# GpSimd makes the lower part of eleven expert weights, and three float32 units become split ones

## The chip, the core and the metric

The kernel runs on one core of a Trainium2 chip. The metric is the time of one execution on the device, in microseconds (us). TensorE multiplies matrices, VectorE and ScalarE do elementwise work, GpSimd is a fourth compute engine, and SyncE issues the transfers. Each engine works through its own instructions in a fixed order and waits at semaphores for the others.

## The reference, cut to what matters

Two transformer blocks over 256 tokens of width 1024, in float32. The change lies in the feed-forward part of the first block, a product-key mixture of 16384 experts:

```python
def chunk(xc):                       # 128 tokens
    q = (xc @ w_query).reshape(128, 8, 2, 128)
    s1 = einsum('thd,hnd->thn', q[:, :, 0], sub_keys_1)
    s2 = einsum('thd,hnd->thn', q[:, :, 1], sub_keys_2)
    v1, i1 = top_k(s1, 16); v2, i2 = top_k(s2, 16)
    cand = v1[..., :, None] + v2[..., None, :]        # 16 x 16 per head
    best, pos = top_k(cand, 16)
    idx = take_along_axis(i1 * 128 + i2, pos)         # experts chosen
    g = softmax(best)
    act = gelu(einsum('td,thkd->thk', xc, expert_u[idx]))
    return einsum('thk,thkd->td', g * act, expert_v[idx])
```

## The kernel before, in words

The kernel gathers nothing. It computes x @ u for all 16384 experts, in 64 units of 256 experts (`unit_u`, line 544 on: the u units), builds the gate values as a dense matrix out of one-hot products, and multiplies the gated activations with all of expert_v.

A matmul in full float32 precision is had in two ways. `wstat` (line 230 on) takes weights that are split into an upper part, which is the weight rounded to float32r, and a lower part, which is the rest, also as float32r. It does three matmuls for each of 16 blocks: upper by upper activations, upper by lower activations, lower by upper activations (lines 240 to 242), 48 in all. `wstat_f32` (line 245 on) uses the unsplit weight in 32 float32 matmuls (line 252) on the float32 activations `xf`, and no other engine works for it.

The split is `load_split` (line 68): a 1 MB transfer on SyncE's queue into one of three buffers `w` (line 71), a copy on ScalarE that makes the upper part (line 77), and a subtraction on VectorE that makes the lower part (line 78). Upper and lower parts have two buffers each, shared by query weights and u units in turn, so the split of a weight waits until the weight two before it has been used up. `load_ahead` does the split earlier than its use, `fetch` takes what lies ready.

The selection stage follows the first block's attention. For each of eight heads `query(h)` does: a 1 MB query weight q by `wstat`, ScalarE copies the result (qT), one u unit, the scores against the keys (sc, line 607), a copy of them to SBUF (scs, lines 613 to 615). `select(h - 1, ...)` then finds the previous head's top 16 on VectorE by max, find and replace steps (lines 583 to 587), adds up the candidates (cand, line 624) and takes the top 16 again. Head 1 has a float32 unit (u0); heads 2 to 7 have split ones (u1 to u6).

The tail of the stage, behind the loop: unit u7 (float32), u8 (split), the last `select`, index arithmetic on VectorE and ScalarE (pi, pf, ij: lines 650 to 658), u9 (split), and for each half of the tokens a lookup by comparison (lines 666 to 671: ScalarE broadcasts `eq`, VectorE compares, multiplies and adds up in a tree), each followed by a float32 unit (u10, u11). A softmax lies between. Then the indices are transposed (tsel, line 684), and 16 steps follow that each take one split u unit (u12 on) and build one-hot tiles on VectorE (oh, lines 706 to 709) for the one-hot matmuls (gp, line 714).

What sets the order: the text of the kernel gives each instruction a priority, earlier text first; a planner runs through them ahead of time with costs of its own, gives each engine the first instruction in priority that is ready then, and so fixes the order on each engine. An instruction that is late in the text can therefore stand early on an engine, where the planner saw a gap. GpSimd has no instruction in this stage.

Of the kernel before, what the change touches and what calls it, by code (L numbers as in the profile page):

```python
# [10 lines left out]
F32 = mybir.dt.float32  # L11
# [37 lines left out]
def kernel(ctx: ExitStack, tc: tile.TileContext, A: dict, out: bass.AP):  # L49
    nc = tc.nc  # L50
    V, S, PE, GP = nc.vector, nc.scalar, nc.tensor, nc.gpsimd
# [10 lines left out]
    def mm_tile(name):  # L62
        return mmp.tile([P, 512], F32, tag="mm", name=name)
# [1 line left out]

    last_split = []

    def load_split(src, n, name, after=(), dst=None):

        w = strm.tile([P, 2048], F32, tag="w", name=name, bufs=3)  # L70
        nc.sync.dma_start(w[:, :n], src)
        hi, lo = dst or [strm.tile([P, 2048], F32R, tag="w" + z, name=f"{name}{z[0]}") for z in ("hi", "lo")]
        with ExitStack() as queued:
            for i in after:
                queued.enter_context(tc.issue_after(i.ins))
            last_split[:] = [
                S.activation(hi[:, :n], w[:, :n], AF.Copy),  # L77
                V.tensor_sub(lo[:, :n], w[:, :n], hi[:, :n].bitcast(F32)),  # L78
            ]
        return hi, lo  # L80

# [89 lines left out]

    ahead = {}

    def load_ahead(src, n, name, after=(), dst=None):
        if name not in ahead:
            ahead[name] = load_split(src, n, name, after, dst)

    def queued(after, f, *a, **kw):

# [5 lines left out]
    def fetch(src, n, name):  # L185
        return ahead.pop(name) if name in ahead else load_split(src, n, name)
# [43 lines left out]
    def wstat(xh, xl, src, name, pool=mm_tile, at=None):  # L230

        hi, lo = fetch(src, 2048, name)
        ps = pool(name + "p")
        for j in range(2):
            for k in range(8):
                if at is not None and j == 0 and k == 4:
                    at()
                c = slice(k * 256 + j * P, k * 256 + j * P + P)
                o = ps[:, j * T : j * T + T]
                PE.matmul(o, hi[:, c], xh[:, k], start=k == 0, stop=False)  # L240
                PE.matmul(o, hi[:, c], xl[:, k], start=False, stop=False)
                PE.matmul(o, lo[:, c], xh[:, k], start=False, stop=k == 7)
        return ps

    def wstat_f32(xf, src, name):

        w = strm.tile([P, 2048], F32, tag="w", name=name, bufs=3)
        nc.sync.dma_start(w, src)
        ps = mm_tile(name + "p")
        for j in range(2):  # L250
            for k in range(8):
                PE.matmul(ps[:, j * T : j * T + T], w[:, k * 256 + j * P : k * 256 + j * P + P], xf[:, k], start=k == 0,
                          stop=k == 7)
        return ps
# [278 lines left out]
    with tc.tile_pool(name="p2", bufs=1) as p2, tc.tile_pool(name="gdram", bufs=1, space=bass.MemoryType.DRAM) as gdp:  # L533
# [7 lines left out]
        gact = {}  # L541
        nu = [0]

        def unit_u(n=1, xf=None):
            for _ in range(n):
                j = nu[0]
                if j == 64:
                    return
                nu[0] += 1
                ps = wstat(xh, xl, A["eu"][j], f"u{j}") if xf is None else wstat_f32(xf, A["eu"][j], f"u{j}")  # L550
                g = p2.tile([P, 512], F32, tag="ga", name=f"ga{j}", bufs=NG)
                S.activation(g, ps, AF.Gelu)
                gact[j] = g

        p2x = tc.tile_pool(name="p2x", bufs=1)
        xf = p2x.__enter__().tile([P, 8, T], F32, name="xf")
        with tc.tile_pool(name="p2a", bufs=1) as p2a:
            rs_f, pr = [], []

            def normed_x():  # L560

                rs_f.append(n_f.end())
                dg = p2a.tile([P, 2, P], F32, name="dgf")
                for t in range(2):
                    V.tensor_scalar(dg[:, t], ident, rs_f[0][:, t : t + 1], None, OP.mult)
                for k in range(8):
                    pt = mm_tile(f"ptn{k}")
                    for t in range(2):
                        PE.matmul(pt[:, t * P : t * P + P], x[t][:, k * P : k * P + P], dg[:, t], start=True, stop=True)
                    S.activation(xf[:, k], pt[:, :T], AF.Copy, scale=gcols[:, G_FFN + k : G_FFN + k + 1])  # L570

            def split_x():
                for k in range(0, 8, 2):
                    S.activation(xh[:, k : k + 2], xf[:, k : k + 2], AF.Copy)
                    V.tensor_sub(xl[:, k : k + 2], xf[:, k : k + 2], xh[:, k : k + 2].bitcast(F32))
# [13 lines left out]
            def query(h):  # L589
                ps = wstat(xh, xl, A["w_query"][h], f"q{h}", at=(lambda: pr.extend(n_f.half(1))) if h == 0 else None)  # L590
                if h == 0:
                    load_ahead(A["w_query"][1], 2048, "q1", pr)
                keys = p2a.tile([P, 2, P], F32, tag="keys", name=f"keys{h}", bufs=2)
                nc.sync.dma_start(keys, A["keys"][h])
                qT = p2a.tile([P, 512], F32, tag="qT", name=f"qT{h}", bufs=2)
                S.activation(qT, ps, AF.Copy)
                if h == 0:
                    normed_x()
                elif h == 1:
                    unit_u(1, xf)  # L600
                    split_x()
                else:
                    unit_u()
                s = mm_tile(f"sc{h}")
                for t in range(2):
                    for f in range(2):
                        PE.matmul(s[:, (2 * t + f) * P : (2 * t + f + 1) * P],
                                  qT[:, f * T + t * P : f * T + t * P + P], keys[:, f], start=True, stop=True)
                sc = p2a.tile([P, 4, P], F32, tag="sc", name=f"scs{h}", bufs=2)
                s = s.rearrange("p (a b) -> p a b", a=4)  # L610
                if h < 2:
                    for t in range(2):
                        S.activation(sc[:, 2 * t : 2 * t + 2], s[:, 2 * t : 2 * t + 2], AF.Copy, scale=rs_f[0][:, t : t + 1])
                else:
                    S.activation(sc, s, AF.Copy)
                return sc

            def select(h, sc):
                for t in range(2):
                    for f in range(2):  # L620
                        top16(sc[:, 2 * t + f], vals[:, t, f, h], idxu[:, t, f, h])
                cand = p2a.tile([P, 2, 112], F32, tag="cand", name=f"cand{h}", bufs=2)
                for o, i0, ni, nj in ((0, 0, 4, 16), (64, 4, 12, 4)):
                    V.tensor_tensor(
                        cand[:, :, o : o + ni * nj].rearrange("p t (i j) -> p t i j", i=ni),
                        vals[:, :, 0, h, i0 : i0 + ni].unsqueeze(3).to_broadcast((P, 2, ni, nj)),
                        vals[:, :, 1, h, 0:nj].unsqueeze(2).to_broadcast((P, 2, ni, nj)), OP.add)
                for t in range(2):
                    top16(cand[:, t], best[:, t, h], posu[:, t, h])

            prev = None
            for h in range(8):
                sc = query(h)
                if prev is not None:
                    select(h - 1, prev)
                prev = sc
            unit_u(1, xf)
            unit_u(1)
            select(7, prev)


# [14 lines left out]
            for a in range(2):  # L656
                V.tensor_mul(pf[2 + a], pf[2 + a], pf[4])
                V.tensor_add(ij[a].rearrange("p t h k -> p (t h k)"), pf[a], pf[2 + a])
            unit_u(1)
            sel = [pf[2 + f].rearrange("p (t h k) -> p t h k", t=2, h=8) for f in range(2)]  # L660
            iota16 = p2a.tile([P, 16], BF16, name="iota16")
            V.tensor_copy(iota16, iota[:, 0:16])
            for t in range(2):
                for f in range(2):
                    eq = p2a.tile([P, 8, 16, 16], BF16, tag="eq", name=f"eq{t}{f}", bufs=2)
                    S.activation(eq, ij[f][:, t].unsqueeze(3).to_broadcast((P, 8, 16, 16)), AF.Copy)
                    V.tensor_tensor(eq, iota16.unsqueeze(1).unsqueeze(1).to_broadcast((P, 8, 16, 16)), eq, OP.is_equal)
                    V.tensor_tensor(eq, eq, idxb[:, t, f].unsqueeze(2).to_broadcast((P, 8, 16, 16)), OP.mult)
                    for w in (8, 4, 2):
                        V.tensor_add(eq[:, :, :, 0:w], eq[:, :, :, 0:w], eq[:, :, :, w : 2 * w])  # L670
                    V.tensor_add(sel[f][:, t], eq[:, :, :, 0], eq[:, :, :, 1])
                unit_u(1, xf)

            eb = pf[0].rearrange("p (t h k) -> p t h k", t=2, h=8)
            V.tensor_tensor(eb, best, best[:, :, :, 0:1].to_broadcast((P, 2, 8, 16)), OP.subtract)
# [75 lines left out]
    with tc.tile_pool(name="p3", bufs=1) as p3:  # L751
# [13 lines left out]
        def p4(name, bufs=2, tag=None):  # L765
            return p3.tile([P, 4, P], F32, tag=tag or name[:-1], name=name, bufs=bufs)
# [281 lines left out]
        for t in range(2):  # L1048
# [5 lines left out]
            u = p4(f"uu{t}", tag="am")  # L1054
# [5 lines left out]
            w = p4(f"wT{t}", tag="vb")  # L1060
# [460 lines left out]
```

## Time and profile before

| | us |
|---|---|
| median of 3 runs | 1744.41 (1744.34 to 1745.78) |
| the profiled execution | 1744.05 |
| its span, first to last instruction | 1742.3 |

| engine | busy us | share of the span |
|---|---|---|
| TensorE, matmul | 1700.4 | 98% |
| TensorE, weight load | 1491.7 | 86% |
| VectorE | 1130.6 | 65% |
| ScalarE | 883.8 | 51% |
| GpSimd | 22.9 | 1% |

The shares are averages over stages with different limits. The selection stage with its loop over heads lies at about 208 to 341 us of the span. PE is TensorE, PEld its weight loads, DVE VectorE, ACT ScalarE, POOL GpSimd. A row of a timeline gives the start and the duration in us, the engine, the line of the kernel, the operation, what is written and read, and in brackets how long the engine was idle before it and what ended that.

### The profile page before, as it was taken

What the parts mean: (1) busy time and instruction counts of PE and PEld (TensorE: products, weight loads), DVE (VectorE), ACT (ScalarE), POOL (GpSimd) and SP (SyncE); (2) the same over time, 40 slices, a digit from 0 to 9 for tenths busy, and PEclk for the clock granted to TensorE, in tenths of its full rate; (3) what the DMA queues carried; (4) which work ended last, traced back from release to release, by engine and by line L of the source; (5) the groups of instructions that cost most, each with busy time, mean ns of one, the idle gap of its engine ahead of it and who ended that gap; (6) DMA issues with size and microseconds to landing.
All of it is one profiled execution on the core that took longest, in us unless ns stands there. A gap on an engine that the chain in (4) does not pass through costs nothing.

```text
span 1742.3 us, 26306 instructions
## 1 busy us (share of the span) xinstructions
PE 1700.4 (98%) x10702; PEld 1491.7 (86%) x10702; DVE 1130.6 (65%) x1924; ACT 883.8 (51%) x1156; POOL 22.9 (1%) x22
## 2 busy tenths in 40 slices
PE   8999999999999999999999999989999999999998
PEld 7788899899998888899888887878999787788896
DVE  6645699999656566555555588666555677765555
ACT  5664544555444444444444469445444557544444
POOL 0000000000000000000000000001000001100000
PEclk9999999999999999999999999999999999999999
DMA  6324544477777777765555553224555553345552
GB/s 240 136 103 145 179 155 165 175 272 289 252 262 247 244 244 245 247 220 193 190 180 186 193 175 122 97 74 159 194 194 190 178 174 126 113 169 193 177 186 97
DMA packets 83066, 321.40 MB, mean 184 GB/s; under 512 B 9472, under 2 KB 44544, under 8 KB 47104
## 3 DMA queue, kind: packets, MB, share of 16 engines
q1 hardware_dynamic: 82944, 319.71, 53.2%
q8 instruction: 84, 1.38, 0.3%
q14 instruction: 38, 0.31, 0.0%
HBM read 301.85 MB, written 17.83 MB: 183 GB/s over the span
## 4 chain that ended last, share of the span: by engine, by line
PE 88%; DVE 7%; ACT 4%; issue 1%; DMA 1%; SPq 0%; DVEq 0%; ACTq 0%
PE pv L85 7%; PE pv L83 7%; PE pv L84 7%; PE m L85 3%; PE m L84 3%; PE m L83 3%; PE gp L714 2%; PE wia L84 1%; PE wia L85 1%; PE wia L83 1%; PE pt L92 1%; PE pj L1181 1%; PE wda L85 1%; PE wda L83 1%; PE wda L84 1%
## 5 line engine op out<-in xcount | busy, mean ns | idle before, releaser
L737 ACT ACTIVATE wh<-ga 128x512 fp32r<-128x512 f32 x64 | 40.4, 632 | 194.8 <-PE pv L84 194.8
L738 DVE TENSOR_TENSOR wl<-ga,wh 128x512 fp32r<-128x512 f32 x64 | 44.2, 692 | 91.0 <-ACT wh L737 91.0
L1201 ACT ACTIVATE ah<-mr 128x512 fp32r<-128x512 f32 x32 | 20.2, 631 | 76.8 <-DVE mr L1198 76.8
L709 DVE TENSOR_TENSOR oh<-oh,gT 128x1024 f16<-128x1024 f16 x64 | 42.2, 685 | 5.0 <-PE gp L714 5.0
L734 DVE TENSOR_TENSOR ga<-ga,gt 128x512 f32<-128x512 f32 x64 | 41.1, 685 | 3.6 <-DMA gt<-gd 3.5
L1202 DVE TENSOR_TENSOR al<-mr,ah 128x512 fp32r<-128x512 f32 x32 | 22.2, 693 | 21.6 <-ACT ah L1201 21.6
L717 ACT ACTIVATE stg<-gp 128x512 f32<-128x512 f32 x64 | 32.9, 607 | 0.0
L714 PE MATMUL gp<-oh,oh 128*128 128x128 f16 x512 | 32.6, 219 | 0.0
L714 PEld LDWEIGHTS <-oh 128*128 128x128 f16 x512 | 29.4, 97 | 0.9
L92 PE MATMUL pt<-c,x 128*128 128x128 f32 x128 | 21.6, 295 | 6.9 <-DMA x<-x 5.3
L92 PEld LDWEIGHTS pt<-c,x 128*128 128x128 f32 x128 | 16.1, 150 | 12.1 <-issue 6.4
L78 DVE TENSOR_TENSOR wiw_0l<-wiw,wiw_0h 128x2048 fp32r<-128x2048 f32 x7 | 16.0, 2292 | 13.2 <-ACT wiw_0h L77 13.2
L84 PE MATMUL wia<-wiw_0l,gh 128*128 128x512 f32 x56 | 22.6, 404 | 0.1
L100 ACT ACTIVATE gh<-pt,gcols 128x256 fp32r<-128x256 f32 x32 | 13.0, 476 | 18.8 <-PE pt L92 18.8
L85 PE MATMUL wia<-wiw_0h,gl 128*128 128x512 f32 x56 | 22.5, 401 | 0.0
L83 PE MATMUL wia<-wiw_0h,gh 128*128 128x512 f32 x56 | 22.3, 404 | 0.0
L83 PE MATMUL wia<-wiw_1h,gh 128*128 128x512 f32 x56 | 22.0, 392 | 0.0
L85 PE MATMUL wia<-wiw_1h,gl 128*128 128x512 f32 x56 | 21.9, 392 | 0.0
L84 PE MATMUL wia<-wiw_1l,gh 128*128 128x512 f32 x56 | 21.9, 392 | 0.0
L706 DVE TENSOR_TENSOR oh<-iotaR,i1T 128x1024 f16<-128x1024 f16 x32 | 21.9, 684 | 0.0
L1198 DVE TENSOR_TENSOR mr<-mr 128x512 f32<-128x512 f32 x32 | 21.9, 683 | 0.0
L78 DVE TENSOR_TENSOR wdw_0l<-wdw,wdw_0h 128x2048 fp32r<-128x2048 f32 x6 | 13.8, 2292 | 11.9 <-ACT wdw_0h L77 11.9
(2944 smaller groups left out, 6671.2 us busy)
## 6 DMA issues: line engine op xcount, KB each, us to landing
u<-eu SPq DMA_DIRECT2D x64, 1024.0 KB, 5.0
v<-ev SPq DMA_DIRECT2D x64, 1024.0 KB, 4.9
m<-w_mlp SPq DMA_DIRECT2D x64, 1024.0 KB, 4.9
gd<-stg SPq DMA_DIRECT2D x16, 1024.0 KB, 3.9
gt<-gd SPq DMA_DIRECT2D x256, 64.0 KB, 4.4
wiw<-w_in SPq DMA_DIRECT2D x14, 1024.0 KB, 5.2
wdw<-w_qkv SPq DMA_DIRECT2D x12, 1024.0 KB, 4.8
q<-w_query SPq DMA_DIRECT2D x8, 1024.0 KB, 5.0
```

Of the source, the lines that this page charges most:

```text
L78: V.tensor_sub(lo[:, :n], w[:, :n], hi[:, :n].bitcast(F32)),
L83: PE.matmul(o, ah, bh, start=start, stop=False)
L84: PE.matmul(o, ah, bl, start=False, stop=False)
L85: PE.matmul(o, al, bh, start=False, stop=stop)
L92: PE.transpose(pt[:, t * P : t * P + P], src[t][:, k * P : k * P + P], ident)
L709: V.tensor_tensor(oh[2 + i], oh[1], tok(gT[i]), OP.mult)
L714: PE.matmul(ps[:, i * P : i * P + P], oh[0][:, 2 * g + i // 2, :, i % 2], oh[2 + m][:, 2 * g + i // 2, :, i % 2], start=m == 0, stop=m == 1)
L717: S.activation(stg[:, :, c : c + 4], ps.rearrange("p (t n) -> p n t", t=4), AF.Copy, scale=2.0 ** -15)
L734: V.tensor_tensor(w4, w4, gts[q][:, :, 2 * jj : 2 * jj + 2, :].rearrange("p g j t -> p j g t"), OP.mult)
L737: S.activation(wh, w, AF.Copy)
L738: V.tensor_sub(wl, w, wh.bitcast(F32))
L1202: V.tensor_sub(al, r, ah.bitcast(F32))
```

## The change

`load_split` and `load_ahead` get a parameter for the engine of the subtraction. `unit_u` calls `load_ahead` with GpSimd where it is told so, right in front of `wstat`, which then takes the split weight: in the loop over heads from head 2 on (u1 to u6), behind the loop (u7, u8), behind the index arithmetic (u9), and after each half of the lookup (u10, u11). u7, u10 and u11, which were float32 units, thereby become split units with 48 float32r matmuls. u0 stays a float32 unit. The query weights and the units from u12 on keep VectorE. Their transfers stay on SyncE's queue.

```diff
-    def load_split(src, n, name, after=(), dst=None):
+    def load_split(src, n, name, after=(), dst=None, E=V):
 ...
                 S.activation(hi[:, :n], w[:, :n], AF.Copy),
-                V.tensor_sub(lo[:, :n], w[:, :n], hi[:, :n].bitcast(F32)),
+                E.tensor_sub(lo[:, :n], w[:, :n], hi[:, :n].bitcast(F32)),
 ...
-    def load_ahead(src, n, name, after=(), dst=None):
+    def load_ahead(src, n, name, after=(), dst=None, E=V):
         if name not in ahead:
-            ahead[name] = load_split(src, n, name, after, dst)
+            ahead[name] = load_split(src, n, name, after, dst, E)
 ...
-        def unit_u(n=1, xf=None):
+        def unit_u(n=1, xf=None, E=None):
+
             for _ in range(n):
                 j = nu[0]
                 if j == 64:
                     return
                 nu[0] += 1
+                if E is not None:
+                    load_ahead(A["eu"][j], 2048, f"u{j}", E=E)
                 ps = wstat(xh, xl, A["eu"][j], f"u{j}") if xf is None else wstat_f32(xf, A["eu"][j], f"u{j}")
 ...
                 else:
-                    unit_u()
+                    unit_u(E=GP)
 ...
                 prev = sc
-            unit_u(1, xf)
-            unit_u(1)
+            unit_u(2, E=GP)
             select(7, prev)
 ...
                 V.tensor_add(ij[a].rearrange("p t h k -> p (t h k)"), pf[a], pf[2 + a])
-            unit_u(1)
+            unit_u(1, E=GP)
 ...
                     V.tensor_add(sel[f][:, t], eq[:, :, :, 0], eq[:, :, :, 1])
-                unit_u(1, xf)
+                unit_u(1, E=GP)
```

## Rows read from the trace of the kernel before

**Rows 1.** The page's busy time by engine: us, share of the span, instructions.
```profile
PE 1700.4 (98%) x10702; PEld 1491.7 (86%) x10702; DVE 1130.6 (65%) x1924; ACT 883.8 (51%) x1156; POOL 22.9 (1%) x22
```

**Rows 2.** Windows: length, busy PE, PEld, DVE, ACT, POOL, then clock, DMA share, GB/s.
```profile
219.70:341.30 121.60, 118.11 (x913) 113.73 (x912) 114.38 (x439) 55.64 (x56) 0.00 (x0) 1.00 0.48 170
...
341.30:480.00 138.70, 138.70 (x1431) 137.83 (x1430) 119.09 (x146) 77.27 (x103) 0.00 (x0) 1.00 0.73 264
...
302.00:336.00 34.00, 32.17 (x199) 29.33 (x198) 33.61 (x94) 19.16 (x20) 0.00 (x0) 1.00 0.59 207
...
345.00:352.50 7.50, 7.50 (x81) 7.34 (x80) 7.50 (x11) 4.18 (x7) 0.00 (x0) 1.00 0.70 257
```

**Rows 3.** Timeline of TensorE, selection stage: two matmuls behind idle time.
```profile
252.29 0.39 PE L242 MATMUL q4p<-gh,q4l 128*128 128x256 f32 x1 [0.83 <-DVE q4l L78]
...
336.00 0.33 PE L684 MATMUL tsel<-c,pf 128*128 128x128 f32 x1 [1.58 <-DVE pf L671]
```

**Rows 4.** Timeline of TensorE, tail of the stage: where units and gp begin.
```profile
300.87 7.07 PE L252 MATMUL u7p<-xf,u 128*128 128x256 f32 x32
307.59 0.47 PE L240 MATMUL u8p<-gh,u8h 128*128 128x256 f32 x1
...
318.67 7.07 PE L252 MATMUL u10p<-xf,u 128*128 128x256 f32 x32
325.58 7.07 PE L252 MATMUL u11p<-xf,u 128*128 128x256 f32 x32
...
341.27 1.10 PE L714 MATMUL gp<-oh,oh 128*128 128x128 f16 x16
```

**Rows 5.** Timeline of VectorE, tail of the stage.
```profile
302.00 2.29 DVE L78 TENSOR_TENSOR u9l<-u,u9h 128x2048 fp32r<-128x2048 f32 x1
304.21 0.48 DVE L583 MAX8 vals<-scs 128x8 f32<-128x128 f32 x2
...
311.88 0.49 DVE L650 TENSOR_SCALAR pi<-posu 128x256 int32<-128x256 int32 x2
...
315.95 2.29 DVE L78 TENSOR_TENSOR u12l<-u,u12h 128x2048 fp32r<-128x2048 f32 x1
...
326.38 2.23 DVE L78 TENSOR_TENSOR u13l<-u,u13h 128x2048 fp32r<-128x2048 f32 x1
328.53 1.21 DVE L667 TENSOR_TENSOR eq<-iota,eq 128x2048 bf16<-128x2048 bf16 x1
```

**Rows 6.** Timelines of ScalarE and TensorE: unit u2, then the tail.
```profile
238.44 1.92 ACT L77 ACTIVATE u2h<-u 128x2048 fp32r<-128x2048 f32 x1 [3.04 <-PE u1p L241]
...
240.74 0.59 ACT L615 ACTIVATE scs<-sc 128x512 f32<-128x512 f32 x1
...
244.94 0.28 PE L242 MATMUL u2p<-gh,u2l 128*128 128x256 f32 x1
...
302.35 0.59 ACT L615 ACTIVATE scs<-sc 128x512 f32<-128x512 f32 x1
...
316.06 3.70 ACT L666 ACTIVATE eq<-ij 128x2048 bf16<-128x2048 bf16 x2
...
325.41 1.91 ACT L666 ACTIVATE eq<-ij 128x2048 bf16<-128x2048 bf16 x1 [0.46 <-DVE pf L671]
```

**Rows 7.** Timeline of GpSimd, in later stages.
```profile
1182.69 3.65 POOL L1254 MEMSET dT<- 64x2048 f32 x2 [127.31 <-PE woea L85]
...
1459.38 3.08 POOL L1339 TENSOR_SCALAR ali<-c1b 128x384 f32<-128x384 f32 x1 [269.31 <-DVE ds01m L296]
1463.52 1.18 POOL L1339 TENSOR_SCALAR ali<-c1b 128x384 f32<-128x384 f32 x1 [1.07 <-DVE dr11z L116]
```

**Rows 8.** Timeline of VectorE beside these GpSimd instructions.
```profile
1459.14 2.29 DVE L78 TENSOR_TENSOR wdw_1l<-wdw,wdw_1h 128x2048 fp32r<-128x2048 f32 x1
...
1463.70 0.37 DVE L115 TENSOR_TENSOR dr11z<-dr11y 128x16 f32<-128x16 f32 x1
...
1464.52 0.18 DVE L115 TENSOR_TENSOR dr11z<-dr11y 128x16 f32<-128x16 f32 x1
```

## The prediction

> **What bounds the kernel now.** I read the page's busy shares first, then the table of windows, then the idle times of TensorE in the stage, then each engine's timeline from 290 to 345 us. TensorE is busy for 98% of the span [rows 1]. In the selection stage (219.7 to 341.3 us) it is busy 118.11 of 121.6 us, and from the first matmul of the one-hot product (gp, 341.27) to 480 us for all of the 138.7 [rows 2]. So any move of that first gp matmul, with the same units u0 to u12 done before it, goes into the time one for one, unless new idle time opens behind it. Of the 3.49 us idle, two waits of 0.83 (one row stands) are for a lower part of a query weight made by VectorE, and 1.58 is for the end of VectorE's selection arithmetic [rows 3]. VectorE is busy 33.61 of 34 us between 302 and 336, GpSimd not at all [rows 2]. The stage is thus bound by two engines: TensorE in the loop over heads, VectorE's chain in the tail behind it.
>
> **The change part by part.**
>
> TensorE's work. Units 7, 10 and 11 go from 32 float32 matmuls to 48 float32r ones. A float32 unit takes 325.58 - 318.67 = 6.91 us; two float32r units take 318.67 - 307.59 = 11.08, so 5.54 each [rows 4]. That is 3 x 1.37 = 4.1 us less work. It counts only where TensorE is the bound.
>
> VectorE's work. The lower parts of u1 to u6, u8 and u9 leave it: eight subtractions of 2.29 us with a pitch of 2.2 [rows 5]. In the loop over heads this lets the selection of a head start when its scores are copied (240.74 + 0.59 = 241.33 [rows 6]) and not after u2l, and the query part behind it comes out earlier by more than the 0.83 us that TensorE waits: both waits go, -1.66 us.
>
> ScalarE. Three more upper parts (u7, u10, u11) of 1.9 us; it is busy 19.16 of 34 us in the tail [rows 2], so there is room, but each can stand ahead of a broadcast (eq) by up to 1.9 us. I take 0 and keep that in the range. The loads are issued in the same order on the same SyncE queue, three slots deep; a slot of raw weights now comes free when GpSimd has read it, and I price that at nothing: the load that needs the slot has more than a unit (5.5 us) to land.
>
> GpSimd's subtraction, two inputs of 128x2048, is in no row. The nearest are the eight scalings of 128x384, one input [rows 7]: 1.18 us where nothing is in the way. A small VectorE product that began 0.18 us behind that scaling took 0.37 us and not 0.18 [rows 7, 8]: it got on 0.37 us after GpSimd's start, long before the scaling's end. So reading 384 columns takes about 0.37 us (0.96 ns a column) and 0.81 is fixed. Two inputs of 2048 would be 2 x 2048 x 0.96 = 3.9 + 0.8 = 4.7 us. The lower bound is the 64x2048 memset at 1.82 us for one stream [rows 7]; twice that stream and the fixed part is 1.8 x 2 + 0.8 = 4.4; all of the scaling's time in proportion gives 1.18 x 2048/384 = 6.3, and 12.6 if the second input costs as much again. I take 4.6, between the two that separate a fixed part, and keep 1.8 and 12.6 as far ends. [...]
>
> Does that fit the loop? u2's upper part is ready at 240.36 and the first matmul on its lower part starts at 244.94 [rows 6]: 4.58 us. With 4.6 and some 0.1 for the hand-over each of u2 to u6 waits 0.1 us, 0.5 in all; u1 has a whole unit more. The loop so ends 1.66 - 0.5 = 1.2 us earlier. A matmul that waits for GpSimd holds all of TensorE's queue, the scores of the head among it; GpSimd itself has nothing else queued. If it took 6.3, five waits of 1.8 would come (rival 2).
>
> The tail, by VectorE's chain. The last selection begins at 304.21, behind u8l and u9l; its scores are there at 302.35 + 0.59 = 302.94 [rows 5, 6]. Now it can start at 302.94 - 1.2 = 301.7: **-2.5 us**. u13l (2.2 us) stands in the chain in front of a comparison whose input was ready at 327.32; the comparison began at 328.53 [rows 5, 6]: **-1.2 us**, as u13 has no slot that early any more (two slots for split weights, which u10 and u11 now take). u12l filled a wait for ScalarE (316.06 to 317.96 [rows 6]) but for 0.2 us; it needs u10's slot now, and the next such wait is about as long: **+0.3 us**.
>
> What comes in is the price for sharing. Where a VectorE subtraction of two SBUF inputs began 0.24 us before a scaling on GpSimd, the scaling took 3.08 us and ended 1.03 us after VectorE was done (1459.38 + 3.08 against 1459.14 + 2.29) [rows 7, 8]. So the two engines exclude each other, and the later one waits. In the loop GpSimd's 4.6 us fall beside max, find and replace steps of one input, and the pair of candidate sums comes about 1 us later. In the tail they don't. Counting from u7's start at 300.87 - 1.2 = 299.7 [rows 4], a unit every 5.5 us, an upper part of 1.9 us after each freed slot, and GpSimd holding VectorE off for its 3.9 us of reading: u9l from 307.1 to 311.0, against index arithmetic that would start at 309.3 (301.7 plus the 7.67 us from 304.21 to 311.88 [rows 5]): 1.7 us, if its first steps, of one input, are held too, which no row shows. u10l from 312.8 to 316.7, in the midst of that arithmetic (4.07 us long, to 315.95 [rows 5]): 3.9. u11l from 319.0 to 322.9, against the first comparison, ready at 321.0: 1.9. Together **+7.5 us**, between 0 (no exclusion) and 3 x 4.7 = 14.1 (all three in full, fixed part too).
>
> [...]
>
> So the first gp matmul moves by -2.5 - 1.2 + 0.3 + 7.5 = +4.1 us, to 345.4. TensorE would be there with u12 done at about 336 (five units from 299.7 with two waits of about 1 us for GpSimd end at 329, then u12 and the transposes): it loses all that it saved, waiting for VectorE. Behind it VectorE has 2.2 us more to do (u13l), and it is busy 7.50 of 7.50 us in the first steps after 345 [rows 2] but less later; I take half, +1.1. The sum is +5.2.
>
> The sum is against the profiled execution, 1744.05 us (span 1742.3 and 1.75 around it); the median of the three runs is 0.36 higher. 1744.05 + 5.2 = 1749.25, with that 0.36 about **1749.5 us**.
>
> **The rivals.**
>
> 1. The engines don't hold each other up as I say, or only for moments, and VectorE's relief arrives. For it: the small VectorE products from 1463.70 on ran beside a scaling with only the first delayed [rows 8]. Against: the scaling of 3.08 us. The 7.5 goes, and the sum is -2.5 - 1.2 + 0.3 + 1.1 = -2.3, so 1742.1: not slower. It decides if the three waits are together under 2.3 us. TensorE's own limit (u12 done at 336 and not at 341.3) would allow -5.3, no more.
>
> 2. The subtraction on GpSimd takes 6.3 us or more. Then u2 to u6 wait 1.8 us each (9 us where I had 0.5), and the hold in the tail grows by some 1.6 us for each of three units: 5.2 + 8.5 + 4.8 = +18.5, so 1763. For it: the only timed GpSimd arithmetic in proportion. Against: the 0.37 us. It decides above 4.58 us, by 5 us a microsecond.
>
> 3. The planner, which writes each engine's order ahead, puts other work into the gap: u13 ahead of the first gp matmuls on TensorE. For it: u12l and u13l stand amid the selection arithmetic today [rows 5]. Against: u13's slot is free only when u11 ends, near 329, and VectorE is in its chain then. The 5.5 us of u13 would fill the wait: 5.2 - 5.5 = -0.3, so 1744.1.
>
> **How the numbers follow.** My forecast 0.43, with its own range 1746 to 1754 (waits of 4 to 12 us); rival 1 0.33, 1738.5 to 1744; rival 2 0.12; rival 3 0.12. Faster or slower means by over 0.2%, 3.5 us, about what a measurement of this kernel can tell from no change: below 1740.9, above 1747.9. Slower: three quarters of the forecast (0.32) and rival 2, 0.44. Faster: half of rival 1 (0.17) and a quarter of rival 3, 0.20. The rest, 0.36, is the same. The range takes in rival 1 and leaves most of rival 2 outside: 1738.5 to 1756.
>
> **What would show it.** In the profile after: GpSimd subtractions of 4.4 to 4.8 us in the loop (right), over 5 us there with waits "GpSimd u" before the third matmul of each unit (rival 2). Query waits of 0.83 us gone. In the tail, comparisons and index steps on VectorE that last 2 to 5 us where they lasted 0.3 to 1.2, each ending with a GpSimd read; the first gp matmul near 345, with TensorE idle some 8 us before it. Wrong would be: those VectorE steps at their old durations beside running GpSimd subtractions, or the first gp matmul before 341.3.

## The result and the profile after

The changed kernel takes 1757.38 us (median of 4 runs, 1756.18 to 1758.46), the kernel before 1745.1 on the same chip. The ratio is 1.0072, with a 95% interval of 1.0058 to 1.0085: slower by 12 us, where 1749.5 was forecast and the range ended at 1756. The direction was right, the size was not.

The profiled execution of the changed kernel took 1756.18 us, its span is 1754.4, 12.1 more than before. First the page's busy times by engine, to be read against [rows 1]:

```profile
PE 1701.6 (97%) x10750; PEld 1493.8 (85%) x10750; DVE 1127.1 (64%) x1916; ACT 888.2 (51%) x1159; POOL 74.1 (4%) x33
```

The totals hardly move: GpSimd has 51 us more, VectorE 3.5 less, though eight subtractions of 2.29 us, 18 us in all, have left it. Much of the difference is VectorE steps that were held, which count as busy: 8.9 us in the tail, shown below, and 2.3 in the loop. The table of windows of the changed kernel says where the time went (length, busy PE, PEld, DVE, ACT, POOL, granted clock, DMA share, GB/s):

```profile
218.30:300.00 81.70, 81.39 (x679) 79.59 (x678) 62.53 (x327) 36.71 (x37) 32.47 (x8) 1.00 0.48 165
300.00:318.00 18.00, 15.84 (x135) 15.25 (x134) 14.98 (x65) 9.94 (x12) 12.53 (x3) 1.00 0.47 169
318.00:325.00 7.00, 5.79 (x36) 5.79 (x37) 6.96 (x3) 4.45 (x5) 5.32 (x2) 0.76 0.44 150
325.00:336.00 11.00, 7.74 (x65) 7.26 (x63) 10.51 (x17) 5.20 (x4) 0.95 (x1) 1.00 0.26 95
336.00:340.00 4.00, 1.23 (x3) 0.69 (x3) 3.96 (x7) 4.00 (x4) 0.00 (x0) 0.58 0.00 0
340.00:350.00 10.00, 6.90 (x29) 6.32 (x30) 10.00 (x16) 0.47 (x1) 0.00 (x0) 0.50 0.31 107
350.00:352.50 2.50, 2.50 (x23) 2.46 (x22) 1.66 (x3) 0.00 (x0) 0.00 (x0) 0.94 0.40 69
352.50:480.00 127.50, 127.49 (x1335) 126.63 (x1334) 111.04 (x137) 72.71 (x99) 0.00 (x0) 1.00 0.76 273
```

In the loop over heads (to 300) VectorE has time to spare now. From 300 to 352.5 us TensorE is busy 40.0 of 52.5 us: 12.5 us idle where it was 3.49 over the whole stage, and its granted clock, 1.00 all through the stage before [rows 2], is 0.76 from 318 to 325 and 0.50 from 340 to 350. Behind 352.5 it is busy to the last as before.

What held TensorE is seen by pairing GpSimd's timeline with VectorE's. GpSimd in the tail of the changed kernel:

```profile
306.14 4.60 POOL L78 TENSOR_TENSOR u9l<-u,u9h 128x2048 fp32r<-128x2048 f32 x1 [1.74 <-ACT u9h L77]
314.48 4.68 POOL L78 TENSOR_TENSOR u10l<-u,u10h 128x2048 fp32r<-128x2048 f32 x1 [3.73 <-ACT u10h L77]
320.83 5.12 POOL L78 TENSOR_TENSOR u11l<-u,u11h 128x2048 fp32r<-128x2048 f32 x1 [1.68 <-ACT u11h L77]
```

and VectorE beside it, which answers to [rows 5]:

```profile
300.71 0.49 DVE L586 MAX8 vals<-scs 128x8 f32<-128x128 f32 x2 [4.70 <-ACT scs L618]
...
308.39 2.70 DVE L652 TENSOR_SCALAR pi<-posu 128x256 int32<-128x256 int32 x2
311.02 0.28 DVE L654 CAST pf<-posu 128x256 f32<-128x256 int32 x1
...
316.71 3.53 DVE L669 TENSOR_TENSOR eq<-iota,eq 128x2048 bf16<-128x2048 bf16 x1 [1.96 <-ACT eq L668]
320.27 1.22 DVE L670 TENSOR_TENSOR eq<-eq,idxb 128x2048 bf16<-128x2048 bf16 x1
321.41 5.62 DVE L669 TENSOR_TENSOR eq<-iota,eq 128x2048 bf16<-128x2048 bf16 x1
...
342.03 2.28 DVE L78 TENSOR_TENSOR u12l<-u,u12h 128x2048 fp32r<-128x2048 f32 x1
344.24 0.41 DVE L688 CAST i2T<-tsel 128x256 f16<-128x256 f32 x1
...
346.37 1.28 DVE L711 TENSOR_TENSOR oh<-oh,gT 128x1024 f16<-128x1024 f16 x2
```

The same comparisons, and the last one-hot step that the first gp matmul needs, in the kernel before:

```profile
318.15 1.22 DVE L667 TENSOR_TENSOR eq<-iota,eq 128x2048 bf16<-128x2048 bf16 x1
...
320.55 1.22 DVE L667 TENSOR_TENSOR eq<-iota,eq 128x2048 bf16<-128x2048 bf16 x1
...
339.97 1.28 DVE L709 TENSOR_TENSOR oh<-oh,gT 128x1024 f16<-128x1024 f16 x2
```

Add starts and durations: u9l ends at 310.74, u10l at 319.16, u11l at 325.95. The three long VectorE steps start while GpSimd runs and end at 311.09, 320.24 and 327.03, that is 0.35, 1.08 and 1.08 us behind those moments, no more than they need by themselves. They last 2.70, 3.53 and 5.62 us where they lasted 0.49, 1.22 and 1.22: holds of 2.2, 2.3 and 4.4 us, 8.9 together (by a hold I mean the time that a VectorE step lasts longer beside a GpSimd instruction). Each hold runs to the end of the GpSimd instruction. It works the other way too: u11l itself took 5.12 instead of 4.6, since it began beside a VectorE product that ended at 321.49.

On TensorE's timeline in the changed kernel this arrives as a row of waits, and behind the last of them u12 still has nearly all its matmuls to do:

```profile
319.21 0.38 PE L242 MATMUL u10p<-gh,u10l 128*128 128x256 f32 x1 [2.70 <-POOL u10l L78]
...
334.64 0.44 PE L686 MATMUL tsel<-c,best 128*128 128x128 f32 x2 [2.35 <-ACT ga L555]
338.30 0.48 PE L686 MATMUL tsel<-c,pf 128*128 128x128 f32 x1 [3.22 <-DVE pf L673]
...
342.17 0.47 PE L686 MATMUL tsel<-c,pf 128*128 128x128 f32 x1 [0.85 <-DVE pf L673]
344.37 0.58 PE L242 MATMUL u12p<-gh,u12l 128*128 128x256 f32 x1 [1.73 <-DVE u12l L78]
344.96 0.42 PE L241 MATMUL u12p<-gl,u12h 128*128 128x256 f32 x1
347.94 0.42 PE L240 MATMUL u12p<-gh,u12h 128*128 128x256 f32 x1
350.65 0.29 PE L242 MATMUL u12p<-gh,u12l 128*128 128x256 f32 x1
352.26 0.28 PE L241 MATMUL u12p<-gl,u12h 128*128 128x256 f32 x1
352.49 0.69 PE L716 MATMUL gp<-oh,oh 128*128 128x128 f16 x9
```

VectorE's tiles for the first gp matmul are ready at 346.37 + 1.28 = 347.65; that matmul starts at 352.49. Before, they were ready at 339.97 + 1.28 = 341.25 and it started at 341.27 [rows 4]. Fourteen matmuls lie between the row at 344.96 and the one at 347.94, 0.213 us each, and fourteen between 350.65 and 352.26, 0.115 each: at the granted clock of 0.50 u12 goes at about half its pace.

The runs of the kernel before that were timed beside the experiments lie between 1740.2 and 1750.3 us, the low ones with a mean granted clock of 1.000, the high ones with 0.993. So for the experiments I also give, from each trace, the **stage**: from u0's first matmul to the last of the one-hot product, the stretch in which every kernel here works off the same units, u0 to u27 (some of them float32 units in one kernel and split in another, 6.9 us of TensorE against 5.5). It is read to about 0.1 us from one trace of each kernel. It is 237.0 us before (219.7 to 456.7) and 249.5 in the changed kernel (218.3 to 467.8): +12.5, which is the whole loss.

### The profile page after: what moved, and what is told of

It reads as the page before. It is cut to its first block, busy times and chain, and to the rows that moved or that the text cites. A ratio compares the mean times of both kernels' runs of the same rounds, so it can differ in the third digit from the quotient of the medians.

```text
span 1754.4 us, 26416 instructions
## 1 busy us (share of the span) xinstructions
PE 1701.6 (97%) x10750; PEld 1493.8 (85%) x10750; DVE 1127.1 (64%) x1916; ACT 888.2 (51%) x1159; POOL 74.1 (4%) x33
## 4 chain that ended last, share of the span: by engine, by line
PE 85%; DVE 7%; ACT 4%; issue 2%; POOL 1%; DMA 0%; SPq 0%; DVEq 0%; ACTq 0%; POOLq 0%
PE pv L85 7%; PE pv L83 7%; PE pv L84 7%; PE m L85 3%; PE m L84 3%; PE m L83 3%; PE gp L716 2%; PE wia L84 2%; PE wia L85 2%; PE wia L83 1%; PE pt L92 1%; DVE eq L669 1%; PE pj L1183 1%; PE wda L85 1%; PE wda L84 1%
## 5 line engine op out<-in xcount | busy, mean ns | idle before, releaser
L1341 POOL TENSOR_SCALAR ali<-c1b 128x384 f32<-128x384 f32 x8 | 16.6, 2076 | 284.7 <-DVE ds01m L296 269.3
L586 DVE MAX8 vals<-scs 128x8 f32<-128x128 f32 x32 | 7.6, 280 | 22.6 <-ACT scs L618 18.3
```

## The experiments

Ten kernels; the first four ran beside the kernel before at 1745.86 us, the next four at 1744.03, the last two at 1742.76.

| kernel | time, us | ratio to before (95%) | stage | first gp after u0's start |
|---|---|---|---|---|
| before | | | 237.0 | 121.6 |
| changed | 1757.38 | 1.0072 (1.0058 to 1.0085) | 249.5 | 134.2 |
| 1 VectorE and float32 units in the tail | 1748.04 | 1.0017 (1.0000 to 1.0034) | 238.5 | 123.4 |
| 2 GpSimd in the tail alone | 1759.67 | 1.0078 (1.0055 to 1.0102) | 247.1 | 131.4 |
| 3 fills of zeros on GpSimd | 1759.73 | 1.0079 (1.0055 to 1.0103) | 249.8 | 134.7 |
| 4 u12 a float32 unit | 1754.97 | 1.0055 (1.0039 to 1.0071) | 245.9 | 131.0 |
| 5 no lower part for u1 to u11 | 1744.62 | 1.0005 (0.9989 to 1.0022) | 237.5 | 122.4 |
| 6 u12 ahead in the order | 1756.22 | 1.007 (1.0048 to 1.0091) | 247.4 | 135.3 |
| 7 tail split by VectorE | 1753.81 | 1.0066 (1.004 to 1.0091) | 244.1 | 128.8 |
| 8 tail in float32, u12 early | 1746.44 | 1.0011 (0.9997 to 1.0025) | 238.1 | 122.4 |
| 9 GpSimd up to u9 | 1747.84 | 1.0028 (1.0014 to 1.0042) | 239.2 | 123.9 |
| 10 GpSimd in the loop alone | 1743.24 | 1.0 (0.9986 to 1.0014) | 237.1 | 121.7 |

The intervals of the times tell numbers 1, 5, 8, 9 and 10 from the changed kernel, and numbers 2, 3, 4, 6 and 7 from the kernel before, but those five not from the changed kernel. What is said below of differences among them, and between them and the changed kernel, is read from one trace each.

**1 and 2: is it the loop or the tail?** In the first, GpSimd keeps u1 to u8, VectorE splits u9 (the first line), and u10 and u11 are float32 units again:

```
-            unit_u(1, E=GP)
+            unit_u(1)
...
-                unit_u(1, E=GP)
+                unit_u(1, xf)
```

> The change without its tail: u1 to u8 on GpSimd (u7 a split unit), u9 split on VectorE, u10 and u11 float32 units as in the kernel before. Theory A: no GpSimd subtraction lies beside the index arithmetic; the loop's two waits of 0.83 us stay away, the last selection starts 3.5 us earlier, u12 and u13 are split ahead again, so 1739 to 1743 us, faster than before. If the GpSimd subtractions in the loop cost something themselves, or the slots matter and not the reads: 1745 us or more.

The second is the reverse: the loop, u7 and u8 as before, GpSimd for u9, u10 and u11.

```
-                    unit_u(E=GP)
+                    unit_u()
...
-            unit_u(2, E=GP)
+            unit_u(1, xf)
+            unit_u(1)
```

> The tail of the change alone: u1 to u8 as in the kernel before (VectorE, u7 float32), u9, u10 and u11 on GpSimd. Theory A: all of the loss is here, and the loop's gains are gone: 1757 to 1761 us. If the loss comes from the loop or from u7 and u8: 1744 to 1748 us.

The stage is 238.5 us in the first and 247.1 in the second, which came in at 1759.67 as expected: the loss is in the tail. The first missed its time all the same: 11 of the 12.5 us come back, but the gain that I expected of the loop isn't there. In the second the holds fall elsewhere. u9l runs from 301.78 to 306.31 beside max and find steps and holds nothing; u10l (319.91 to 325.49) and u11l (332.95 to 337.89) hold four tree steps and a product, which take 1.66 and 1.22 us by themselves:

```profile
321.06 5.97 DVE L673 TENSOR_TENSOR eq<-eq 128x512 bf16<-128x512 bf16 x4
...
333.44 5.54 DVE L671 TENSOR_TENSOR eq<-eq,idxb 128x2048 bf16<-128x2048 bf16 x1
```

That is 8.6 us in sum, near the 8.9 of the changed kernel, at other steps.

**3: does GpSimd hold VectorE by reading?** For u1 to u11 GpSimd fills the lower part with zeros instead of subtracting, three and a half times 1.8 us each.

```
-                E.tensor_sub(lo[:, :n], w[:, :n], hi[:, :n].bitcast(F32)),
+                E.tensor_sub(lo[:, :n], w[:, :n], hi[:, :n].bitcast(F32)) if E is V else E.memset(lo[:, :n].bitcast(F32), 0.0),
             ]
+            if E is not V:
+                for m in (n, n, n // 2):
+                    E.memset(lo[:, :m].bitcast(F32), 0.0)
```

> The changed kernel, but on GpSimd the lower part of u1 to u11 is not computed: it writes zeros in its place, in three and a half fills of about 1.8 us (about as long as wait for the upper part plus subtraction), which read nothing from SBUF. Left out of the computation: the lower weight parts of eleven units. Buffers, slots and matmuls stay. Theory A (the subtraction's reads shut VectorE out for 8.9 us in the tail, and all that is late follows from it): VectorE's steps of 2.70, 3.53 and 5.62 us go back to 0.5 and 1.2, ScalarE's queue is no longer held by a broadcast, the first gp matmul comes at 338 to 342 and the time is 1741 to 1747 us. Theory B (u10 and u11 take the two slots for split weights, so u12's split is late whatever the engines do): first gp matmul at 348 or later, 1752 us or more.

The expectation that fills leave VectorE alone fell. GpSimd's timeline in this kernel, and VectorE's beside it:

```profile
307.95 4.88 POOL L82 MEMSET u9l<- 128x2048 f32 x3
312.77 1.95 POOL L78 MEMSET u10l<- 128x2048 f32 x1
314.78 4.78 POOL L82 MEMSET u10l<- 128x2048 f32 x3
```

```profile
306.24 0.44 DVE L630 TENSOR_TENSOR cand<-vals 128x128 f32<-128x128 f32 x2
306.60 1.57 DVE L648 CAST idxb<-idxu 128x512 bf16<-128x512 uint32 x1
...
312.89 1.98 DVE L657 CAST pf<-posu 128x256 f32<-128x256 int32 x1
314.90 1.87 DVE L658 TENSOR_SCALAR pf<-pf 128x256 f32<-128x256 f32 x1
316.69 3.01 DVE L655 TENSOR_SCALAR pi<-posu 128x256 int32<-128x256 int32 x2
319.62 0.41 DVE L659 SCALAR_TENSOR_TENSOR pf<-pf,pf 128x256 f32<-128x256 f32 x1
```

The steps held here are of one input: the same CAST and TENSOR_SCALAR last 0.28 and 0.29 us in the changed kernel, and here 1.98 and 1.87, to 314.87 and 316.77; a fill ends at 314.72 and, with 1.8 us each, the next at about 316.6. The two-input steps at 306.24 and 319.62, with a fill beside them, take their 0.44 and 0.41. So the fills here hold other steps than the subtractions did, pi apart, for 9 us in sum as it happens (pi 2.1 and 2.5, the two CASTs 1.2 and 1.7, the TENSOR_SCALAR 1.6). The times of theory B came out (first gp at 352.5, 1759.73 us), but with the holds still there they don't speak for it. As a test of whether the holds cause the loss this kernel says nothing, and number 5 took its place.

**4: does u12's lateness cost by itself?** u12 becomes a float32 unit, which needs neither a slot nor ScalarE nor VectorE.

```
-                unit_u(1)
+                unit_u(1, xf if b == 0 else None)
```

> The changed kernel, but unit u12 is a float32 unit (32 matmuls on the unsplit weight, no split). Theory A in its second half (u12's upper part stands on ScalarE behind two broadcasts, so its lower part comes at 342 and its 48 matmuls run after VectorE's chain, half of them at the lower clock): u12's 6.9 us now run under the chain, the first gp matmul comes when VectorE's one-hot tiles are there, at 344 to 347 instead of 352.5, and the time is 1749 to 1752 us. If VectorE's chain alone set the end: no change, 1756 to 1758. If the float32 matmuls only cost their 1.4 us more: 1758 to 1759.

The stage shrinks by 3.6 us and the time by 2 to 3, about half of what was expected. u12 starts when TensorE's queue lets it, at 338.65 behind the waits of 2.51 and 3.22 us for the transposes, and runs 14 of its 32 matmuls at 0.36 us each, the others at 0.21. VectorE's tiles are ready 130.2 us after u0, no earlier than in the changed kernel (u13l stands there now), but the first gp matmul comes 0.8 us behind them where it was 4.8. Two causes were still mixed: u12's place, and the 2.2 us that its subtraction takes from VectorE.

**5: with no GpSimd at all, and the rest unchanged.** The lower parts of u1 to u11 aren't made; slots, upper parts and 48 matmuls a unit stay.

```
-            last_split[:] = [
-                S.activation(hi[:, :n], w[:, :n], AF.Copy),
-                E.tensor_sub(lo[:, :n], w[:, :n], hi[:, :n].bitcast(F32)),
-            ]
+            last_split[:] = [S.activation(hi[:, :n], w[:, :n], AF.Copy)]
+            if E is not V:
+                return hi, hi
+            last_split.append(V.tensor_sub(lo[:, :n], w[:, :n], hi[:, :n].bitcast(F32)))
```

> For u1 to u11 the lower part isn't made at all: nothing runs on GpSimd in the stage, and the matmuls that read the lower part read the upper one again (the lower part of these weights is left out). The upper parts, their slots, their place in ScalarE's order and the 48 matmuls of each unit stay. Theory A (GpSimd's holds on VectorE, 2.2 + 2.3 + 4.4 us, start everything; that ScalarE then has u12's upper part stuck behind a broadcast, and the lower clock, follow from them): the steps of 2.70, 3.53 and 5.62 us go back to 0.5 and 1.2, TensorE idles under 4 us in the tail, the first gp matmul comes 117 to 121 us after u0's start (134.2 after the change, 121.6 before), time 1740 to 1746. Theory B (three more split units in two slots, with ScalarE's order, are enough for the loss): gp 128 us or more after u0's start, time 1750 or more.

The stage falls from 249.5 to 237.5 us, and the time to that of the kernel before: GpSimd's subtractions are where the loss starts. This kernel also lacks TensorE's waits for them, 0.61 us before u9's third matmul and 2.70 before u10's in the changed kernel. Those can't make the loss by themselves: there TensorE is done with u11 at 331.9 and then waits for ScalarE and VectorE, and VectorE's chain from the first comparison to the tiles has one wait, of 0.35 us, for ScalarE, and none for TensorE. So what counts of the two is the holds. VectorE in number 5:

```profile
308.72 0.50 DVE L652 TENSOR_SCALAR pi<-posu 128x256 int32<-128x256 int32 x2
...
314.18 1.23 DVE L669 TENSOR_TENSOR eq<-iota,eq 128x2048 bf16<-128x2048 bf16 x1 [1.30 <-ACT eq L668]
...
316.58 1.22 DVE L669 TENSOR_TENSOR eq<-iota,eq 128x2048 bf16<-128x2048 bf16 x1
```

The first gp matmul comes 122.4 us after u0, a little later than the 117 to 121 expected. The loop alone is 2.3 us shorter here than before (below), but TensorE waits 2.5 us for u10's upper part, which ScalarE makes behind two broadcasts. So the three more split units cost something in ScalarE's order as well; it is small against the holds.

**6: u12 earlier, with the holds as they are.** u12 is split ahead of the second pair of comparisons and stands in TensorE's queue ahead of the transposes.

```
-                    S.activation(eq, ij[f][:, t].unsqueeze(3).to_broadcast((P, 8, 16, 16)), AF.Copy)
+                    queued(u12[:1], S.activation, eq, ij[f][:, t].unsqueeze(3).to_broadcast((P, 8, 16, 16)), AF.Copy)
...
-                unit_u(1, E=GP)
+                unit_u(1 + t, E=GP if t == 0 else None)
+                if t == 0:
+                    load_ahead(A["eu"][11], 2048, "u11", E=GP)
+                    load_ahead(A["eu"][12], 2048, "u12")
+                    u12[:] = last_split
...
-                unit_u(1)
+                unit_u(min(b, 1))
```

> The changed kernel, GpSimd's subtractions and their holds as they are; but u12 is split ahead of the second pair of comparisons: ScalarE makes u12's upper part before the broadcast that waits for VectorE, and TensorE has u12 in its queue ahead of the transposes of the selection. Theory A (the holds make VectorE's chain 8.9 us longer, and ScalarE's order makes u12 late on top, which TensorE then runs behind the chain and at half clock): u12 runs straight behind u11, the first gp matmul comes when VectorE's one-hot tiles are ready, 129 to 130.5 us after u0's start, and the time is 1751.5 to 1754. Rival (the place of u12 is of no account, since TensorE has it to do anyway): 1756 to 1759. Rival (the place of u12 is all of the loss): 1743 to 1747.

My theory gave 1751.5 to 1754, the rival 1756 to 1759, and 1756.22 was measured, in the rival's range, though the interval (1.0048 to 1.0091) takes in both. The first gp matmul decides: 135.3 us after u0 and not 129 to 130.5, so my theory failed. VectorE's timeline in this kernel shows why:

```profile
333.82 2.28 DVE L78 TENSOR_TENSOR u12l<-u,u12h 128x2048 fp32r<-128x2048 f32 x1
336.02 1.22 DVE L670 TENSOR_TENSOR eq<-iota,eq 128x2048 bf16<-128x2048 bf16 x1
...
345.20 2.28 DVE L78 TENSOR_TENSOR u13l<-u,u13h 128x2048 fp32r<-128x2048 f32 x1
...
347.74 2.29 DVE L78 TENSOR_TENSOR u14l<-u,u14h 128x2048 fp32r<-128x2048 f32 x1
349.94 0.69 DVE L713 TENSOR_TENSOR oh<-iotaR,i1T 128x1024 f16<-128x1024 f16 x1
```

u12 runs before the transposes, as meant. But each unit that goes ahead takes 2.2 us of VectorE first, and here u13l and u14l as well stand ahead of the one-hot steps. The stage gains 2.1 us of the 12.5. While VectorE is the engine that is late, TensorE work that needs VectorE doesn't fill TensorE's wait for it. In number 4 u12 needed none, and its stage is the shorter by 1.5 us.

**7: the same split units, made by VectorE.** The line for u9, and that for u10 and u11 alike:

```
-            unit_u(1, E=GP)
+            unit_u(1, E=V)
```

> u1 to u8 as in the changed kernel; the lower parts of u9, u10 and u11 (48 matmuls each, as there) are made by VectorE, 2.2 us each, and not by GpSimd, 4.6 us each. Theory A (GpSimd holds VectorE for the whole of its 4.6 us): VectorE pays 6.7 us itself instead of 8.9 us of holds, and 1.3 to 2 us of that fall into its waits for ScalarE; u12 still needs u10's slot. First gp matmul 128 to 131 us after u0's start, time 1750 to 1754. Rival (it matters only that three more units are split late, not who does it): as changed, 1756 to 1759. Rival (work in VectorE's order costs nothing beside TensorE): 1742 to 1746.

As expected: the first gp matmul 128.8 us after u0, 1753.8 us. But two things changed at once, as the planner put u12l elsewhere too:

```profile
330.88 2.22 DVE L78 TENSOR_TENSOR u12l<-u,u12h 128x2048 fp32r<-128x2048 f32 x1
...
346.87 1.29 DVE L711 TENSOR_TENSOR oh<-oh,gT 128x1024 f16<-128x1024 f16 x2
```

VectorE's tiles are ready 346.87 + 1.29 - 220.0 = 128.2 us after u0, 1.2 earlier than in the changed kernel. The first gp matmul comes 0.6 us behind them and not 4.8, since u12 is split ahead of the last comparisons here. So of the 5.4 us by which the stage is shorter, some 1.2 come from VectorE subtracting itself, for 2.2 us a unit, in place of being held, and the rest from u12's place. Neither way is as good as float32 units, which need no subtraction.

**8, 9 and 10: is there a part worth keeping?** In 8 GpSimd makes u1 to u8, u9 to u11 are float32 units (u9's line is shown, that of u10 and u11 is alike), and u12 is split early:

```
-            unit_u(1, E=GP)
+            unit_u(1, xf)
+            load_ahead(A["eu"][12], 2048, "u12")
```

> GpSimd makes the lower parts of u1 to u8 alone; u9, u10 and u11 are float32 units without a lower part, and u12 is split by VectorE ahead of the comparisons. If the loop's saving (the two waits of 0.83 us gone, the last selection 2 us earlier) comes through once nothing holds VectorE in the tail: no VectorE step over 2.5 us between 300 and 345 us, first gp matmul 119.5 to 121 us after u0's start, time 1742 to 1745, a little under the kernel before. If the loop's saving is used up by the short waits for GpSimd (0.3 us before the third matmul of u2 to u6), or by VectorE's chain: 121.5 to 123, 1745 to 1748.

In 9 one GpSimd subtraction is left in the tail, u9's; u10 and u11 change:

```
-                unit_u(1, E=GP)
+                unit_u(1, xf)
```

> GpSimd makes the lower parts of u1 to u9; u10 and u11 are float32 units again, so that one GpSimd subtraction is left in the tail, u9's, which held VectorE's first index step for 2.2 us in the changed kernel. If a hold costs VectorE just the overlap (as much here as the 2.2 us of a subtraction of its own): the stage, from u0's first matmul to the last of the one-hot product, is as long as with u9 on VectorE (238.5 us; 237.0 before, 249.5 changed), so 237.5 to 239.5, time 1745 to 1749. Rival (each GpSimd subtraction in the tail costs a third of the loss, some 4 us): 241 us or more, time 1749 or more.

In 10 only the units of the loop over heads, u1 to u6, are on GpSimd, the rest is as before (the edit is to the kernel before, with the parameter that the change adds):

```
-                    unit_u()
+                    unit_u(E=GP)
```

> The kernel before, with only u1 to u6, the units inside the loop over heads, moved to GpSimd; u7, u10 and u11 are float32 units, u8 and u9 are split by VectorE. If the loop's part of the change is a gain by itself: both waits of 0.83 us gone against short waits for GpSimd of 0.3 us in u2 to u6, u7 starts 80 to 80.7 us after u0 (81.2 before), the stage is 235.5 to 236.8 us long (237.0 before), time 0.3 to 1.5 us under the kernel before. Rival (VectorE's chain in the tail sets the end, and the loop's part is lost in it or in the waits for GpSimd): 237 to 239 us, time as before or 1 to 2 us over it.

None beats the kernel before. Number 9 shows the price of a single hold: its first index step lasts 2.70 us again, and the stage is 239.2 us against 238.5 where VectorE made u9l itself, no better than its own 2.2. In 8 and 10 the rival expectation held: nothing comes out of the loop. From u0's first matmul to u7's it takes 81.2 and 80.8 us where VectorE makes the lower parts (before, number 2), 80.2 to 81.2 in the eight kernels where GpSimd subtracts, and 78.9 with no lower part at all (number 5). The changed kernel's TensorE shows what uses the gain up:

```profile
243.42 0.28 PE L241 MATMUL u2p<-gl,u2h 128*128 128x256 f32 x1
243.76 0.39 PE L242 MATMUL u2p<-gh,u2l 128*128 128x256 f32 x1
243.98 0.28 PE L240 MATMUL u2p<-gh,u2h 128*128 128x256 f32 x1
```

Matmuls follow each other by 0.11 us; here by 0.34 and 0.22, since u2l is ready at 243.71 (239.09 + 4.62). That is 0.33 us for each of u2 to u6, 1.7 in all, as much as the two waits of 0.83 us that are gone; it is too short to be listed as idle time.

## Why the prediction was wrong, step by step

The forecast for the first gp matmul was +4.1 us against u0's start, and +5.2 for the whole; measured are +12.6 and +12.1.

- **TensorE's work.** Right: u11 takes 331.9 - 326.3 = 5.6 us where the float32 unit took 6.91, and nothing comes of it, as TensorE isn't the bound in the tail.
- **GpSimd's subtraction.** Right: 4.6 us, the value taken out of a range from 1.8 to 12.6; rival 2 is out. In part that is luck: the split into 3.9 us of reading and 0.8 fixed, from which the value came, isn't what the holds show, which last to the instruction's end even where the VectorE step began 0.58 us behind it (321.41 against 320.83).
- **The loop, -1.2.** Both waits of 0.83 us are gone; in this trace it is -1.0. The wait for GpSimd was taken as 0.1 us a unit and is 0.33, and over all kernels the gain is nil within 0.5 us.
- **The start of the last selection, -2.5.** 300.71 is 82.4 us after u0; 304.21 was 84.5 [rows 5]: -2.1. **u13l out of the chain, -1.2.** Right: the third comparison starts at 332.72, when ScalarE's broadcast is ready, 0.8 us after the end of the reciprocal (gs) that u13l stood behind; before it was 2.1.
- **The holds, +7.5.** Mechanism right, the size short: 8.9. u9l was to cost 1.7 and cost 2.2, u10l 3.9 and 2.3 (it met a later step than I said, the first comparison), u11l 1.9 and 4.4. That the sum came near is in part luck, as errors of -1.6 and +2.5 us offset each other. I had counted 3.9 us of reading as held and not the whole instruction. The trace shows the whole instruction for the two comparisons, which end 1.08 us behind the ends of GpSimd's 4.68 and 5.12. With the 0.8 us that I had taken as fixed counted in each of the three waits, this term would have been 2.4 more, 9.9 where 8.9 was measured. Rival 1, no exclusion, is out.
- **u12l in the next wait for ScalarE, +0.3.** Failed. u12's upper part needs u10's slot, free when u10's matmuls end at about 326.4. By then the wait that u12l filled before was over: it stands empty in the changed kernel (1.96 us before 316.71), and u12l comes into VectorE's chain in full at 342.03. That is +2.1 (2.2 there, 0.1 less at the first comparison) and not +0.3. Number 6, where u12l stands earlier, pays the same 2.2 at 333.82.
- **"TensorE would be there with u12 done at about 336".** Failed, and this is the largest term: u12 ends at 352.4. VectorE's chain is done 347.65 - 218.3 = 129.35 us after u0 against 341.25 - 219.7 = 121.55, so +7.8; that is my chain with 8.9 for 7.5, 2.1 for 0.3, -2.1 for -2.5, the -1.2 as it was, and 0.1 of small steps. It makes 3.7 of the 8.5 us by which the forecast of the first gp matmul was short. The other 4.8, from the tiles to the first gp matmul, are u12's. Already u11 ended at 331.9, 4.3 us later against u0 than my 329: TensorE waited 0.61 and 2.70 us for GpSimd, where I had two waits of about 1, and ran part of u10 at a lower clock (0.76 over 318 to 325 us). And I treated u12 as TensorE's own work that falls into the wait for VectorE; it needs VectorE itself, and ScalarE, whose queue in the changed kernel has u12's upper part behind a broadcast that waits 8.29 us for VectorE:

```profile
330.77 1.91 ACT L668 ACTIVATE eq<-ij 128x2048 bf16<-128x2048 bf16 x1 [8.29 <-DVE pf L673]
...
336.29 1.90 ACT L77 ACTIVATE u12h<-u 128x2048 fp32r<-128x2048 f32 x1
```

  The slot for it was free at about 326.4; I had entered ScalarE's order at 0.
- **The granted clock** wasn't in the sum at all. After TensorE's idle stretches (2.35, 3.22, 1.00 and 0.85 us between 332 and 342) it was at 0.50 from 340 to 350 us: some 28 of u12's matmuls (344.37 to about 350.3) took 0.213 us and not 0.115, which is 2.7 of those 4.8 us.
- **Behind gp, +1.1.** Nothing: first gp +12.6, last gp +12.5.
- **Rival 3.** u13 wasn't pulled forward but for two matmuls. In number 6 it was, and the first gp matmul came 135.3 us after u0, later than the 134.2 of the changed kernel: it wouldn't have been free.

So the trigger is shown (number 5 against the changed kernel), and its place too (1 and 2). How it works on through VectorE's chain and u12 is read from the rows, whose terms add up to the loss; numbers 4, 6 and 7 agree with it by their traces, not by their times, which can't be told from the changed kernel's. How much of the loss the lower clock makes by itself is only worked out from the rows: no kernel held the clock up while the holds stayed.

## What to carry to other kernels

Work given to GpSimd wasn't free for VectorE here: comparisons, products and index steps stood until GpSimd's subtraction ended, and one of them, 5.12 us long, cost the critical VectorE chain 4.4 us, more than the 2.2 that VectorE would have needed. Look for where such instructions land, and move only those that fall beside steps of VectorE that they don't hold, as the max and find steps here (0.45 us for two max and 0.27 for a find beside u9l, as in the kernel before), or beside its idle time. When a chain gets longer, ask of each piece of work that is to fill the wait which engines prepare it: if one of them is the late one, it fills nothing. And price idle time on TensorE with the clock that follows it, if the trace shows a lower one (0.50 for 10 us here).

## What was not expected of the hardware

- A GpSimd fill, which reads nothing, held VectorE's one-input steps (CAST 0.28 to 1.98 us, TENSOR_SCALAR 0.29 to 1.87) until it ended, and left two-input steps alone (0.41 and 0.44 us). In the changed kernel GpSimd's subtraction held a two-input comparison (1.22 to 3.53 and 5.62) and a one-input step (0.49 to 2.70), while the max, find and replace steps from 306.14 to 308.39, of one input too, ran beside u9l at their usual lengths.
- TensorE's granted clock was 0.58 over the window from 336 to 340 us, in which TensorE was busy 1.23 of 4 us, and 0.50 over all of the next ten, in which it was busy 6.90; it was at 1.00 again from 352.5. So the matmuls behind these waits paid for them too, 0.213 us each and not 0.115. A wait alone doesn't settle it: behind 2.70 us before u10's third matmul the clock was 0.76 over 318 to 325 in the changed kernel, where u10's matmuls last up to 0.42 us; behind 2.7 us at the same place in number 4 they last 0.28, but for one of 0.38. In the kernel before no wait in this stage was followed by a lower clock: there the longest was 1.58 us [rows 3] and the clock stayed at 1.00 [rows 2].
